# One 512-column matmul for hi and lo of the activation, in the second half of a two-block transformer kernel

## The chip, the core and the metric

The kernel runs on one core of one Trainium2 chip. The metric is the device time of one execution in microseconds. The profile is one further execution, taken by the hardware profiler; its span is from the first to the last instruction. Engines are named as in the profile: PE is TensorE's matmuls, PEld its weight loads, DVE is VectorE, ACT ScalarE, POOL GpSimd, SP SyncE.

## What is computed

Two transformer blocks follow each other on 256 tokens of width 1024, all in float32. The first has two attention layers with cross attention to a memory. The second, which the change touches, is cut to this:

```python
def second_block(x, mem, ...):
    x = x + hybrid_mixer(rms_norm(x, g_mix), w_in, conv_w, g_attn_out, g_conv_out, w_out)
    x = x + memory_cross_attention(rms_norm(x, g_xattn), rms_norm(mem, g_mem),
                                   w_q_mem, w_kv_mem, w_o_mem)
    x = x + squared_relu_mlp(rms_norm(x, g_mlp), w_up, w_down)
    return rms_norm(x, g_final)

def hybrid_mixer(h, w_in, conv_w, g_attn_out, g_conv_out, w_out):
    q, k, v, bg, cg, xc = jnp.split(h @ w_in, 6, axis=-1)
    ...
    conv = short_gated_conv(bg, cg, xc, conv_w)
    merged = jnp.concatenate([rms_norm(attn, g_attn_out), rms_norm(conv, g_conv_out)], axis=-1)
    return merged @ w_out

def squared_relu_mlp(h, w_up, w_down):
    a = jax.nn.relu(h @ w_up)
    return (a * a) @ w_down
```

The mixer's attention has 8 heads of 64 and three dilated windows; cross attention has 4 heads of 256 over 256 memory rows; the MLP is 4096 wide.

## The kernel before

**Numbers in two parts.** Every matmul operand is split into hi (the value rounded to the format fp32r) and lo (what is left). A product takes three matmuls, in `mm3` (L421): hi x hi, hi x lo, lo x hi, all added up in one PSUM bank. Weights are loaded in raw pieces (`load`, L408), and `split` (L413) makes hi with a copy on ACT (tile `wh`) and lo with a subtraction on DVE (tile `wl`), four buffers of each.

**Two forms of projection.** `proj_t` (L427) gives the result transposed, features on the partitions and the 256 tokens on the free axis. It covers 256 features as two halves f of 128. For each half and each of the 8 k tiles of 128 input features it does one `mm3` whose stationary operand is a 128x128 tile of weights and whose moving operand is the activation's hi or lo of 256 columns. Both halves lie in one PSUM bank of 128 x 2 x 256, and the consumers read that bank. `proj_n` (L439) takes the activation as stationary operand and weights of up to 512 columns as moving operand; it gives values and outputs with the tokens on the partitions.

**The activation's tiles.** `turns` (L614), `gain_t` (L478) and `layer_even` (L956) make the normed activation, transposed, as hi and lo. Each returns a function of (l, k) that gives hi (l = 0) or lo (l = 1) of k tile k as 128 x 256. The tiles are slots of 4 KB a partition from a common pool of 25 (`SLOTS`), each with four k tiles of one part: tiles `mT`, `gh` and `hT` in the profile.

**The second block.** `mixer` (L1154) first lets `heads8` (L1063) project k and q (4 calls of `proj_t`) and v; then come the three gates of the convolution, 2 x 3 calls, whose results are multiplied, filtered with three taps, squared and normed; the output projection of the convolution's half and that of the attention's half close it. The sum of squares over tokens (`token_rms`, a reduction on DVE and two small matmuls with a vector of ones) stands between the convolution and its residual add. `filling` (L817) holds the keys and values of the second memory, eight steps that are put where TensorE would wait; two key steps run before the mixer, two at its start. `cross` (L1204) calls `proj_t` for four heads. `mlp` (L1252) runs its first block of 512 features with its own loop (`up_first`), the other seven with two calls of `proj_t` each into PSUM banks of the tag "at" (`up`), while `down` adds into four banks of the tag "mm" that stay open to the end.

**What sets the order.** The program is not issued as it is written. `Plan.record` (L83) notes each operation with its dependences and a cost, and `Plan.order` (L162) simulates the engines: at each step the engine that can start first takes the ready operation with the least priority number (its place in the program, with shifts from `SHIFT`). Buffers are handed out in the order of first use. The result is a fixed order for each engine, so all instructions are issued from one helper and carry its line, L284. In PSUM a dependence is on the whole bank; in SBUF on the part that is read. Work that is put off with `later` is stepped by `pace`, which `proj_t` calls after every fourth k tile.

Of the kernel before, what the change touches and what calls it, by code (L numbers as in the profile page):

```python
# [13 lines left out]
ALU = mybir.AluOpType  # L14
AX = mybir.AxisListType

P = 128
S = 256
D = 1024
KT = D // P  # L20
# [9 lines left out]
class Plan:  # L30
# [5 lines left out]
    class Engine:  # L36

        def __init__(self, plan, name):
            self.plan, self.engine = plan, name
# [244 lines left out]
            f(*[self.real(v) for v in args], **{k: self.real(v) for k, v in kwargs.items()})  # L284


class Kernel:

    def __init__(self, ctx, tc, a, out):
        self.tc, self.nc, self.a, self.out = tc, Plan(tc.nc), a, out  # L290

        class Pool:

            def __init__(pool, name, bufs, space=None):
                pool.space = space
                pool.real = ctx.enter_context(tc.tile_pool(name=name, bufs=bufs, **({"space": space} if space else {})))

            def tile(pool, shape, dtype, tag=None, name=None, bufs=1):
                return self.nc.tile(pool, shape, dtype, tag, name, bufs)

        pool = Pool
        self.base = pool("base", 1)
        self.wp = pool("wp", 4)
        self.wk = pool("wk", 2)
        self.bp = pool("bp", SLOTS)
        self.ps = pool("ps", 2, space=bass.MemoryType.PSUM)
        self.dr = pool("dr", 1, space=bass.MemoryType.DRAM)
        self.n = 0
        self.bg = deque()
        self.credit = 0.0  # L310
        self.rate = 0.0

    def name(self, s):
        self.n += 1
        return f"{s}_{self.n}"
# [4 lines left out]
    def slot(self, shape, name, dtype=F32R):  # L320
        return self.bp.tile(shape, dtype, tag="b4", name=self.name(name), bufs=SLOTS)

# [104 lines left out]
    def proj_t(self, w, c0, hT, n=256, tag="mm"):  # L427

        raw = self.load(w, 0, KT, c0, n)
        po = self.psum(tag)  # L430
        for f in range(n // P):
            wh, wl = self.split(raw[:, :, f * P:(f + 1) * P])
            for k in range(KT):
                self.mm3(po[:, f, :], wh[:, k, :], wl[:, k, :], hT(0, k), hT(1, k), k == 0, k == KT - 1)
                if k % 4 == 3:
                    self.pace()
        return po[:, :n // P, :]

    def proj_n(self, pieces, nk, n, hT, banks=None, start=True, stop=True):  # L439

        nc = self.nc
        po = banks or [self.psum("mm", [P, 512]) for _ in range(2)]
        for k0, view in pieces:
            wh, wl = self.split(view)
            for t in range(2):
                ts = slice(t * P, (t + 1) * P)
                for j in range(view.shape[1]):
                    k = k0 + j
                    o = po[t][:, :n]
                    xh, xl = hT(0, k)[:, ts], hT(1, k)[:, ts]  # L450
                    nc.tensor.matmul(o, xh, wh[:, j, :], start=start and k == 0, stop=False)
                    nc.tensor.matmul(o, xh, wl[:, j, :], start=False, stop=False)
                    nc.tensor.matmul(o, xl, wh[:, j, :], start=False, stop=stop and k == nk - 1)
                self.pace()
        return po
# [22 lines left out]
    def gain_t(self, src, key):  # L478

        nc = self.nc  # L480
        tiles = [[self.slot([P, 4, S], "gh") for _ in range(2)] for _ in range(2)]

        def turn(k):
            v, g, h, l = src[k // 4][:, k % 4, :], self.gcol(key, k), f(0, k), f(1, k)
            nc.scalar.activation(h, v, AF.Copy, scale=g)
            nc.vector.scalar_tensor_tensor(l, v, g, h.bitcast(F32), ALU.mult, ALU.subtract)

        f = lambda l, k: tiles[l][k // 4][:, k % 4, :]
        return f, turn

    def spread(self, r, b):

        nc = self.nc
        diag = self.work("p", [P, 2, P], PB)
        pb = self.psum("at")
# [83 lines left out]
    def mem_key(self, h, l, po, m):  # L579

        t = self.work("p", [P, 2, S], PB)
        self.nc.vector.tensor_tensor(t, po, m[2].unsqueeze(1).to_broadcast([P, 2, S]), ALU.mult)
# [23 lines left out]
    def square_sum(self, v, ms):  # L606

        junk = self.work("p", [P, 512], PB)
        self.nc.either(("scalar", "activation", (junk, v, AF.Square), {"scale": 1.0 / 32.0, "accum_out": ms}),
# [4 lines left out]
    def turns(self, tag, halves, key):  # L614

        nc = self.nc
        tiles = [[None, None], [None, None]]

        def turn(c, k2):
            if k2 == 0:  # L620
                for l in range(2):
                    tiles[l][c] = self.slot([P, 4, S], "mT")
            pt = self.psum("at")
            for j in range(2):
                k = 2 * k2 + j
                for t in range(2):
                    nc.tensor.transpose(pt[:, j, t * P:(t + 1) * P], halves[c][:, t, k * P:(k + 1) * P], self.ident)
            for j in range(2):
                k = 2 * k2 + j
                g = self.gcol(key, 4 * c + k)  # L630
                h, l = tiles[0][c][:, k, :], tiles[1][c][:, k, :]
                nc.scalar.activation(h, pt[:, j, :], AF.Copy, scale=g)
                nc.vector.scalar_tensor_tensor(l, pt[:, j, :], g, h.bitcast(F32), ALU.mult, ALU.subtract)

        for c in range(2):
            for k2 in range(2):
                self.later(tag, lambda c=c, k2=k2: turn(c, k2))
        return lambda l, k: tiles[l][k // 4][:, k % 4, :]


    def hilo(self, h, l, po, scale=1.0):
# [63 lines left out]
    def softmax(self, sc, bias=None, sink=None, causal=False):  # L705
# [3 lines left out]
        n = [P, S] if causal else [S, S]  # L709
        p = self.work("p", [P, 2, S], PB)  # L710
        st = self.work("st", [P, 8], 8)
# [39 lines left out]
    def pv_pair(self, ws, vs, causal=False):  # L751
# [4 lines left out]
        for e, ((ph, pl), v) in enumerate(zip(ws, vs)):  # L756
            for k in range(2):
                q = slice(P, S) if causal and k else slice(0, S)
                nc.tensor.matmul(po[:, e, q], v(k), ph[:, k, q], start=k == 0, stop=False)
                nc.tensor.matmul(po[:, e, q], v(k), pl[:, k, q], start=False, stop=k == 1)  # L760
        u = self.work("y", [P, S], YB)
        o = self.work("y", [P, S], YB)
        for e in range(2):
# [16 lines left out]
    def gated(self, y, f, o, g):  # L780
        nc = self.nc
        t = self.work("y", [P, S], YB)
        nc.vector.scalar_tensor_tensor(t, o, 0.5, g[:, f, :], ALU.mult, ALU.mult)
# [124 lines left out]
    def rope(self, tag, po, n, i, rx):  # L908
# [15 lines left out]
        def turn(t):  # L924
            src, r = po[t][:, :n * 64], rs[t]
            z = self.work("p", [P, 8, 64], PB)
            nc.vector.scalar_tensor_tensor(z[:, :n, :], src.rearrange("p (h c) -> p h c", c=64), rx[:, t:t + 1],
# [28 lines left out]
    def layer_even(self):  # L956
        nc, a = self.nc, self.a
# [20 lines left out]
        po = self.proj_n(pieces(), KT, 384, xg)  # L978
# [3 lines left out]
        nc.vector.tensor_tensor(sq[0], sq[0], sq[1], ALU.add)  # L982
        r = self.token_rms(sq[0])
        rb = self.spread(r, self.work("y", [P, S], YB))
        tiles = [[self.slot([P, 4, S], "hT") for _ in range(2)] for _ in range(2)]
        for c in range(2):
            t = self.slot([P, 4, S], "xs", F32)
            for k in range(4):
                nc.vector.scalar_tensor_tensor(t[:, k, :], self.xT[c][:, k, :], self.gcol("norm0", 4 * c + k), rb,
                                               ALU.mult, ALU.mult)  # L990
            for k in (0, 2):
                self.hilo(tiles[0][c][:, k:k + 2], tiles[1][c][:, k:k + 2], t[:, k:k + 2])
        hT = lambda l, k: tiles[l][k // 4][:, k % 4, :]
        self.window_bias()
        vs = []
        for c0 in (128, 256):
# [144 lines left out]
    def token_rms(self, sq):  # L1141

        nc = self.nc
        s = self.work("y", [P, S], YB)
        nc.vector.tensor_reduce(s, sq.rearrange("p r s -> p s r"), AX.X, ALU.add)
# [8 lines left out]
    def mixer(self, hT):  # L1154
# [22 lines left out]
        for i in range(2):  # L1177
# [8 lines left out]
            for f in range(2):  # L1186
                ff = 2 * i + f
                acc = self.work("y", [P, S], YB)
                tap = lambda j: self.gcol("convw", 4 * j + ff)
# [62 lines left out]
    def mlp(self, ms):  # L1252
# [11 lines left out]
        def square(t, f, n, po):  # L1264
            r = self.work("tanh", [P, 2, S], 2)[:, :n]
            nc.scalar.activation(r, po, AF.Relu)
            q = self.work("p", [P, 2, S], PB)[:, :n]
            nc.scalar.activation(q, r, AF.Square)
# [64 lines left out]
    def run(self, upto=99):  # L1333
        a = self.a
        self.consts()
        ms = self.layer_even()
        if upto > 1:
            ms = self.layer_odd(ms)
        if upto > 2:
            ms = self.mixer(ms)  # L1340
        if upto > 3:
            ms = self.cross(ms)

        def store(c):
            cs = slice(512 * c, 512 * c + 512)
            self.nc.sync.dma_start(self.out[0, :, cs].rearrange("(t p) d -> p t d", p=P), self.x[:, :, cs])

        if upto > 4:
            self.mlp(ms)
        else:  # L1350
            for c in range(2):
                store(c)
        seq = self.nc.solve()
        with self.tc.manual_schedule():
            self.nc.issue(seq)
# [6 lines left out]
BIAS = [40, 80, 110, 0, 0]  # L1362
VERBOSE = False
LAG = (3, 1)
SLOTS = 25
YB = 5
PB = 4
PH = 4
IDLE = [1, 2, 1]
# [79 lines left out]
```

## Time and profile before

| | us |
|---|---|
| median of 3 runs (lowest to highest) | 787.56 (786.85 to 789.11) |
| the profiled execution | 786.07 |
| its span | 784.3 |
| mixer's main stretch, in the span | 390 to 490 |
| cross attention | 510 to 572 |
| MLP from the second block of features on | 600 to 784 |
| mean granted TensorE clock | 0.997 of full speed |

How to read it: a busy time is the time in which at least one instruction of a group was under way. Matmuls overlap each other, so the "mean ns" of a matmul is its latency from issue to last result; the price of one more in a stream is the distance from one start to the next, seen in the timeline or in long runs of the chain of waits. A group's row gives out<-in by tile names, partitions x elements, the count, busy time and mean, and then the idle time before. Idle time of an engine on which nothing waits costs nothing.

### The profile page before, as it was taken

How to read it: one execution, taken by the hardware profiler on the slowest of the kernel's cores; microseconds unless marked ns; L12 is line 12 of the kernel's file. 1: busy time of each engine (PE TensorE's matmuls, PEld its weight loads, DVE VectorE, ACT ScalarE, POOL GpSimd, SP SyncE). 2: the span in 40 equal slices, each digit the busy share in tenths (PEclk: the TensorE clock that was granted, in tenths of full speed). 3: DMA queues.
4: the chain of work that ended last, by engine and by line, in shares of the span. 5: the costliest groups of instructions: out<-in, count | busy, mean ns of one | idle time of the engine just before them, and what ended most of it. 6: DMA issues, size and time to landing. Idle time of an engine off the chain costs nothing.

```text
span 784.3 us, 13568 instructions
## 1 busy us (share of the span) xinstructions
PE 769.9 (98%) x5320; PEld 715.2 (91%) x5320; DVE 578.2 (74%) x995; ACT 506.3 (65%) x928; POOL 74.7 (10%) x105
## 2 busy tenths in 40 slices
PE   7999999999999999999999999999999999999996
PEld 7799899888999999997999899799989999999985
DVE  5999988998769779869987788876567554445454
ACT  6687965975668568648785777465456654455452
POOL 0640010000001521132011000100000000000000
PEclk9999999999999999999999999999999999999999
DMA  7795455444468855773456644357435656565631
GB/s 229 243 333 163 161 166 195 151 159 164 161 198 260 220 175 156 196 233 135 151 172 191 187 159 164 107 162 242 161 108 168 201 170 203 171 208 170 205 116 54
DMA packets 109996, 140.60 MB, mean 179 GB/s; under 512 B 3779, under 2 KB 81539, under 8 KB 109932
## 3 DMA queue, kind: packets, MB, share of 16 engines
q1 hardware_dynamic: 104460, 131.64, 52.0%
q0 software_dynamic: 5472, 8.10, 4.6%
q8 instruction: 42, 0.69, 0.4%
q14 instruction: 22, 0.18, 0.1%
HBM read 134.98 MB, written 1.06 MB: 173 GB/s over the span
## 4 chain that ended last, share of the span: by engine, by line
PE 88%; DVE 4%; issue 3%; POOL 2%; DMA 1%; ACT 1%; SPq 0%; POOLq 0%; DVEq 0%; ACTq 0%
PE t_mm L284 66%; PE t_at L284 22%; DVE t_wl L284 1%; POOL t_rrs L284 1%; DMA t_xT<-in_x_t_dram 1%; DVE t_y L284 1%; DVE t_p L284 1%; POOL t_ks L284 1%; DMA t_tanh<-in_onehot_dram 0%; SPq L284 0%; ACT t_wh L284 0%; POOL t_rstd L284 0%; DVE t_gh L284 0%; DVE t_sq L284 0%; ACT t_tanh L284 0%
## 5 line engine op out<-in xcount | busy, mean ns | idle before, releaser
L284 DVE TENSOR_TENSOR t_wl<-t_raw,t_wh 128x1024 fp32r<-128x1024 f32 (+1 forms) x237 | 290.6, 1230 | 144.8 <-ACT t_wh L284 144.2
L284 ACT ACTIVATE t_wh<-t_raw 128x1024 fp32r<-128x1024 f32 (+1 forms) x237 | 249.0, 1055 | 200.1 <-PE t_mm L284 141.8
L284 PE MATMUL t_mm<-t_mT,t_wh 128*128 128x256 f32 x992 | 192.5, 287 | 0.0
L284 PEld LDWEIGHTS t_mm<-t_mT,t_wh 128*128 128x128 f32 x992 | 159.4, 191 | 0.4
L284 PE MATMUL t_mm<-t_mT,t_wl 128*128 128x256 f32 x496 | 141.1, 285 | 0.0
L284 PE MATMUL t_mm<-t_wh,t_yh 128*128 128x512 f32 x288 | 113.6, 395 | 0.0
L284 PE MATMUL t_mm<-t_wl,t_yh 128*128 128x512 f32 x288 | 113.6, 394 | 0.0
L284 PE MATMUL t_mm<-t_wh,t_yl 128*128 128x512 f32 x288 | 113.1, 394 | 0.0
L284 PE MATMUL t_at<-t_mT,t_wh 128*128 128x256 f32 x480 | 97.0, 282 | 0.0
L284 PEld LDWEIGHTS t_mm<-t_mT,t_wl 128*128 128x128 f32 x496 | 95.0, 191 | 0.0
L284 PEld LDWEIGHTS t_at<-t_mT,t_wh 128*128 128x128 f32 x480 | 78.8, 190 | 1.6
L284 PE MATMUL t_mm<-t_wh,t_gh 128*128 128x256 f32 (+2 forms) x256 | 65.6, 339 | 2.5 <-ACT t_wh L284 2.5
L284 PE MATMUL t_at<-t_mT,t_wl 128*128 128x256 f32 x240 | 67.6, 282 | 0.0
L284 PE MATMUL t_mm<-t_hT,t_wh 128*128 128x256 f32 x336 | 66.4, 287 | 0.0
L284 PEld LDWEIGHTS t_mm<-t_wh,t_yl 128*128 128x128 f32 x288 | 54.1, 188 | 10.6
L284 PEld LDWEIGHTS t_mm<-t_wl,t_yh 128*128 128x128 f32 x288 | 54.2, 188 | 10.0
L284 PEld LDWEIGHTS t_mm<-t_wh,t_yh 128*128 128x128 f32 x288 | 54.2, 188 | 9.7
L284 ACT ACTIVATE t_p<-t_p,t_st 128x256 f32<-128x256 f32 (+1 forms) x118 | 55.9, 490 | 7.4 <-DVE t_st L284 7.1
L284 POOL TENSOR_TENSOR t_rstd<-t_rstd,t_mhalf 128x2 f32<-128x2 f32 (+1 forms) x12 | 12.2, 1015 | 477.4 <-DVE t_rstd L284 477.4
L284 PEld LDWEIGHTS t_mm<-t_hT,t_wh 128*128 128x128 f32 x336 | 54.2, 191 | 0.3
L284 PE MATMUL t_mm<-t_gh,t_wh 128*128 128x256 f32 x256 | 51.1, 287 | 0.0
L284 PEld LDWEIGHTS t_mm<-t_wh,t_gh 128*128 128x128 f32 x256 | 44.6, 193 | 6.9 <-ACT t_wh L284 3.5
(173 smaller groups left out, 1317.6 us busy)
## 6 DMA issues: line engine op xcount, KB each, us to landing
t_raw<-in_w_in_odd_dram SPq DMA_DIRECT2D x20, 1024.0 KB, 5.1
t_raw<-in_w_up_dram SPq DMA_DIRECT2D x16, 1024.0 KB, 5.5
t_raw<-in_w_down_dram SPq DMA_DIRECT2D x16, 1024.0 KB, 5.2
t_raw<-in_w_in_dram SPq DMA_DIRECT2D x12, 1024.0 KB, 5.2
t_raw<-in_w_in_even_dram SPq DMA_DIRECT2D x10, 1024.0 KB, 5.2
t_raw<-in_w_mem_kv_dram SPq DMA_DIRECT2D x8, 1024.0 KB, 5.4
t_raw<-in_w_out_even_dram SPq DMA_DIRECT2D x6, 1024.0 KB, 5.0
t_raw<-in_w_out_odd_dram SPq DMA_DIRECT2D x6, 1024.0 KB, 5.1
```

The costliest lines, as they stand in the source:

```text
L284: f(*[self.real(v) for v in args], **{k: self.real(v) for k, v in kwargs.items()})
```

## The change

In the second block the activation's hi and lo lie side by side, 2 x 256 columns, and go through hi of the weights as one matmul of 512 columns; lo of the weights still takes hi of the activation alone, 256 columns. The flag `merge` is set ahead of the mixer, so the first block keeps `mm3`. A half f now fills a whole bank: the first 256 columns hold hi x hi + lo x hi, the other 256 hold hi x lo. ACT copies the second part to SBUF (tile `sum`, two buffers of 128 x 2 x 256), DVE adds the first part to it, and consumers read the sum from SBUF. A call takes two PSUM banks in turn instead of one. The class `Halves` makes the activation's tiles: two k tiles with both parts each, made when first asked for. The pool has one slot less.

```diff
+class Halves:
+    def __init__(self, make):
+        self.make, self.tiles = make, {}
+    def pair(self, k):
+        if k // 2 not in self.tiles:
+            self.tiles[k // 2] = self.make()
+        t = self.tiles[k // 2]
+        return t[:, :, 0, :], t[:, :, 1, :]
+    def __call__(self, l, k):
+        return self.pair(k - k % 2)[l][:, k % 2, :]
+    def both(self, k):
+        self.pair(k - k % 2)
+        return self.tiles[k // 2][:, k % 2].rearrange("p l s -> p (l s)")
...
     def proj_t(self, w, c0, hT, n=256, tag="mm"):
         raw = self.load(w, 0, KT, c0, n)
+        if self.merge:
+            return self.proj_sum(raw, hT, n, tag)
         po = self.psum(tag)
...
+    def proj_sum(self, raw, hT, n, tag):
+        nc = self.nc
+        s = self.work("sum", [P, 2, S], SB)
+        for f in range(n // P):
+            wh, wl = self.split(raw[:, :, f * P:(f + 1) * P])
+            po = self.psum(tag)
+            pf = po.rearrange("p a b -> p (a b)")
+            for k in range(KT):
+                last = k == KT - 1
+                if last:
+                    nc.tensor.matmul(po[:, 0, :], wl[:, k, :], hT(0, k), start=False, stop=False)
+                nc.tensor.matmul(pf, wh[:, k, :], hT.both(k), start=k == 0, stop=last)
+                if not last:
+                    nc.tensor.matmul(po[:, 0, :], wl[:, k, :], hT(0, k), start=False, stop=False)
+                if k % 4 == 3:
+                    self.pace()
+            nc.scalar.copy(s[:, f, :], po[:, 1, :])
+            nc.vector.tensor_tensor(s[:, f, :], po[:, 0, :], s[:, f, :], ALU.add)
+        return s[:, :n // P, :]
...
-        tiles = [[self.slot([P, 4, S], "gh") for _ in range(2)] for _ in range(2)]
+        f = Halves(lambda: self.slot([P, 2, 2, S], "gh"))
...
             ms = self.layer_odd(ms)
+        self.merge = True
...
-SLOTS = 25
+SLOTS = 24
 YB = 5
+SB = 2
```

`turns` and `layer_even` get `Halves` in the same way, for the tiles `mT` and `hT`.

What the change makes of TensorE's order, in the MLP, within a half of 128 features. A row names the PSUM bank's tile, the activation's tile, the weight tile and the columns. Before, two k steps:

```order
L284 MATMUL t_at_7949<-t_mT_7168,t_wh_7939 128x256
L284 MATMUL t_at_7949<-t_mT_7178,t_wh_7939 128x256
L284 MATMUL t_at_7949<-t_mT_7168,t_wl_7947 128x256
L284 MATMUL t_at_7949<-t_mT_7168,t_wh_7939 128x256
L284 MATMUL t_at_7949<-t_mT_7178,t_wh_7939 128x256
L284 MATMUL t_at_7949<-t_mT_7168,t_wl_7947 128x256
```

Now the last four k steps of a half and the first matmul of the next:

```order
L284 MATMUL t_at_7962<-t_mT_7109,t_wh_7943 128x512
L284 MATMUL t_at_7962<-t_mT_7109,t_wl_7953 128x256
L284 MATMUL t_at_7962<-t_mT_7109,t_wh_7943 128x512
L284 MATMUL t_at_7962<-t_mT_7109,t_wl_7953 128x256
L284 MATMUL t_at_7962<-t_mT_7122,t_wh_7943 128x512
L284 MATMUL t_at_7962<-t_mT_7122,t_wl_7953 128x256 x2
L284 MATMUL t_at_7962<-t_mT_7122,t_wh_7943 128x512
L284 MATMUL t_at_7989<-t_mT_7008,t_wh_7967 128x512
```

The two matmuls of hi of the weights (tiles 7168 and 7178 are hi and lo of the activation) have become one of 512 columns; the steps alternate 512 and 256 columns, in the last step lo of the weights comes first, and the next half begins in a bank of its own.

The second place is VectorE at the end of the mixer's convolution, from the last gate (bg) to the sum of squares. `t_y` are the taps' result and its product with the gate, `t_yl` lo of the normed input of the output projection, `t_wl` its weights. Before:

```order
L284 TENSOR_TENSOR t_wl_6092<-t_raw_5899,t_wh_6058 128x1024
L284 TENSOR_TENSOR t_y_6102<-t_mm_6019,t_y_6056 128x256
L284 TENSOR_TENSOR t_y_6107<-t_mm_6019,t_y_6062 128x256
L284 TENSOR_TENSOR t_wl_6112<-t_raw_5899,t_wh_6096 128x1024
L284 SCALAR_TENSOR_TENSOR t_yl_5835<-t_y_6102,t_gT,t_yh_5824 128x256
L284 SCALAR_TENSOR_TENSOR t_yl_5835<-t_y_6107,t_gT,t_yh_5824 128x256
L284 TENSOR_REDUCE t_y_6132<-t_sq_5831 128x256
```

Now:

```order
L284 TENSOR_TENSOR t_sum_5938<-t_mm_5934,t_sum_5938 128x256
L284 SCALAR_TENSOR_TENSOR t_y_5957<-t_tanh_5677,t_gT,t_y_5957 128x256
L284 TENSOR_TENSOR t_wl_5986<-t_raw_5784,t_wh_5943 128x1024
L284 SCALAR_TENSOR_TENSOR t_yl_5699<-t_y_5968,t_gT,t_yh_5686 128x256
L284 TENSOR_TENSOR t_y_5999<-t_sum_5938,t_y_5957 128x256
L284 TENSOR_TENSOR t_wl_6003<-t_raw_5784,t_wh_5976 128x1024
L284 SCALAR_TENSOR_TENSOR t_yl_5699<-t_y_5999,t_gT,t_yh_5686 128x256
L284 TENSOR_REDUCE t_y_6018<-t_sq_5690 128x256
```

The product reads the sum in SBUF and no longer the bank; the add of the second half and the last taps come first, and the two products stand apart, the first of them ahead of these rows.

More of the change, by code (lines that the diff above doesn't have):

```diff
@@ L311, in __init__ @@
         self.rate = 0.0
+        self.merge = False
     def name(self, s):
@@ L486, in turn @@
             nc.vector.scalar_tensor_tensor(l, v, g, h.bitcast(F32), ALU.mult, ALU.subtract)
-        f = lambda l, k: tiles[l][k // 4][:, k % 4, :]
         return f, turn
@@ L616, in turns @@
         nc = self.nc
-        tiles = [[None, None], [None, None]]
+        f = Halves(lambda: self.slot([P, 2, 2, S], "mT"))
         def turn(c, k2):
-            if k2 == 0:
-                for l in range(2):
-                    tiles[l][c] = self.slot([P, 4, S], "mT")
             pt = self.psum("at")
@@ L630, in turn @@
                 g = self.gcol(key, 4 * c + k)
-                h, l = tiles[0][c][:, k, :], tiles[1][c][:, k, :]
+                h, l = f(0, 4 * c + k), f(1, 4 * c + k)
                 nc.scalar.activation(h, pt[:, j, :], AF.Copy, scale=g)
@@ L637, in turns @@
                 self.later(tag, lambda c=c, k2=k2: turn(c, k2))
-        return lambda l, k: tiles[l][k // 4][:, k % 4, :]
+        return f
     def hilo(self, h, l, po, scale=1.0):
@@ L984, in layer_even @@
         rb = self.spread(r, self.work("y", [P, S], YB))
-        tiles = [[self.slot([P, 4, S], "hT") for _ in range(2)] for _ in range(2)]
+        hT = Halves(lambda: self.slot([P, 2, 2, S], "hT"))
         for c in range(2):
@@ L991, in layer_even @@
             for k in (0, 2):
-                self.hilo(tiles[0][c][:, k:k + 2], tiles[1][c][:, k:k + 2], t[:, k:k + 2])
-        hT = lambda l, k: tiles[l][k // 4][:, k % 4, :]
+                self.hilo(*hT.pair(4 * c + k), t[:, k:k + 2])
         self.window_bias()
```

## Prediction

> **What bounds the kernel now.** I read the head of the page first, then the table of waits for TensorE alone, then the busy time by stretches.
>
> ```profile
> span 784.3 us, 13568 instructions
> PE 769.9 (98%) x5320; PEld 715.2 (91%) x5320; DVE 578.2 (74%) x995; ACT 506.3 (65%) x928; POOL 74.7 (10%) x105
> PE 88%; DVE 4%; issue 3%; POOL 2%; DMA 1%; ACT 1%; SPq 0%; POOLq 0%; DVEq 0%; ACTq 0%
> ```
>
> TensorE is busy 98% of the span and is 88% of the chain that ended last. A page's busy time can hide short gaps, so the waits come next:
>
> ```profile
> PE t_mm L284 <- ACT t_wh L284: 2.5, 1, 2.5
> PE t_at L284 <- DVE t_p L284: 2.0, 4, 1.0
> PE t_at L284 <- POOL t_warm L284: 1.3, 1, 1.3
> PE t_at L284 <- DMA t_tanh<-in_onehot_dram: 0.8, 1, 0.8
> PE t_mm L284 <- DVE t_wl L284: 0.6, 2, 0.4
> ```
>
> That is all: 7.2 us in 784. So what shortens TensorE's own stream shortens the kernel, and what only loads another engine costs nothing until TensorE has to wait for it. The stretches that the change touches (columns: length, PE, PEld, DVE, ACT and POOL busy, clock, DMA share, GB/s):
>
> ```profile
> 390.00:490.00 100.00, 100.00 (x766) 96.44 (x764) 81.43 (x167) 72.47 (x151) 7.55 (x11) 1.00 0.59 179
> 510.00:572.00 62.00, 62.00 (x504) 61.23 (x504) 40.00 (x58) 35.70 (x63) 1.28 (x2) 1.00 0.55 179
> 600.00:784.00 184.00, 177.24 (x1132) 160.80 (x1130) 93.70 (x99) 96.74 (x128) 1.82 (x3) 1.00 0.51 166
> ```
>
> Mixer, cross attention, MLP: TensorE full at a granted clock of 1.00, VectorE at 81%, 65% and 51% (in the last row TensorE's missing 6.8 us lie behind its last matmul, at the program's end).
>
> **The change part by part. 1: fewer matmuls.** Three groups of the second half (from 388 us) hold what is paired, the products of hi of the weights with hi and with lo of the activation:
>
> ```profile
> L284 PE MATMUL t_at<-t_mT,t_wh 128*128 128x256 f32 x480 | 97.0, 282 | 0.0
> L284 PE MATMUL t_mm<-t_mT,t_wh 128*128 128x256 f32 x480 | 92.1, 287 | 0.0
> L284 PE MATMUL t_mm<-t_gh,t_wh 128*128 128x256 f32 x64 | 11.9, 285 | 0.0
> ```
>
> These are 1024; the MLP's first block (up_first, 2 x 32) keeps its own loop, so 960 matmuls of 256 columns become 480 of 512. That is 30 calls: 2 of keys, 10 in the mixer, 4 in cross attention, 14 in the MLP, each with two halves of 8 k steps.
>
> The mean ns in these rows are latencies; the price is the distance from start to start. The chain of waits has unbroken runs (start, length, count):
>
> ```profile
> 651.85 4.44 PE t_at L284 x37
> 755.45 16.36 PE t_mm L284 x72
> ```
>
> 256 columns: 4.44/37 = 120 ns. 512 columns: 16.36/72 = 227 ns. Twice 120 is 240, so a matmul carries 240 - 227 = 13 ns that do not grow with its columns, and a pair made one saves 13. The new stream alternates 512 with 256 columns, and the MLP has such stretches already, where the planner wove two products together:
>
> ```profile
> 637.41 0.40 PE L284 MATMUL t_mm<-t_wh,t_yh 128*128 128x512 f32 x1
> 641.30 0.40 PE L284 MATMUL t_mm<-t_wh,t_yl 128*128 128x512 f32 x1
> ...
> 659.99 0.40 PE L284 MATMUL t_mm<-t_wh,t_yh 128*128 128x512 f32 x1
> 663.81 0.39 PE L284 MATMUL t_mm<-t_wh,t_yl 128*128 128x512 f32 x1
> ```
>
> Each time 11 steps of 512 and 256 lie between the two rows: 3.89/11 = 354 ns and 3.82/11 = 347 ns. A k step costs three times 120 = 360 now, so it saves 6 to 13 ns. I take the middle, 10 ns: 480 x 10 = **4.8 us gained** (2.9 to 6.2). Whether the 13 ns belong to the matmul or to loading its weights makes no difference, for both go.
>
> The Trainium skill has a rule against this ("TensorE: Matmul & The Clock Gate", section "Back-to-back issue gap"): start to start is the columns at the array clock plus about 2.5 ns. By it a pair saves 2.5 ns and 480 pairs 1.2 us. The runs above, with 13 ns, do not agree, and the sum goes by them.
>
> **2: two new steps behind each half.** ScalarE copies the lo bank half to SBUF, VectorE adds the other. Nearest rows of the same shape and memories:
>
> ```profile
> L284 ACT COPY t_rb<-t_at 128x256 f32<-128x256 f32 x2 | 0.7, 374 | 0.6 <-PE t_at L284 0.6
> L284 DVE TENSOR_TENSOR t_y<-t_mm,t_y 128x256 f32<-128x256 f32 x4 | 1.5, 419 | 0.2 <-PE t_mm L284 0.2
> L284 ACT ACTIVATE t_p<-t_tanh 128x512 f32<-128x512 f32 x14 | 8.8, 632 | 0.4
> L284 ACT ACTIVATE t_tanh<-t_at 128x512 f32<-128x512 f32 x14 | 8.1, 581 | 0.0
> ```
>
> 60 copies at 374 ns are 22.4 us of ScalarE, 60 adds at 419 ns are 25.1 us of VectorE; consumers that now read SBUF cost ScalarE 632 - 581 = 51 ns more each, some 30 times, 1.5 us. None of it is on TensorE. By stage: the mixer's stretch (with the key calls 12) gains 12 x 2 x 0.419 = 10.1 us of VectorE, 91.5 in a stretch that shrinks by 192 x 10 ns to 98.1: 93%. Cross attention goes to 40.0 + 3.4 of 62, the MLP to 93.7 + 11.7 of 184; those two I put at nothing, with TensorE's stream as their cover. If that cover failed, each call would show its new latency, 0.374 + 0.419 = 0.8 us. Is 93% too much? Stretches of before that were as full:
>
> ```profile
> 50.00:100.00 50.00, 49.07 (x366) 46.25 (x364) 46.13 (x80) 39.99 (x85) 1.63 (x1) 1.00 0.61 194
> 80.00:90.00 10.00, 10.00 (x55) 8.44 (x54) 9.77 (x18) 9.94 (x26) 0.00 (x0) 1.00 0.47 160
> ```
>
> VectorE at 92% over 50 us went with 0.93 us lost by TensorE (some of it start-up), and 10 us at 98% with ScalarE at 99% lost none. Over 100 us that bounds the loss at 0 to 1.9; I take **0.5 us lost**, near the second row since splits run ahead of TensorE by up to four buffers.
>
> **3: the join at the mixer's end.** The one place where TensorE already waits for a chain out of a projection. There the last conv gate is multiplied, squared, summed (VectorE), and TensorE needs the sum:
>
> ```profile
> 488.88 1.22 DVE L284 TENSOR_TENSOR t_wl<-t_raw,t_wh 128x1024 fp32r<-128x1024 f32 x1
> 490.13 0.76 DVE L284 TENSOR_TENSOR t_y<-t_mm,t_y 128x256 f32<-128x256 f32 x2
> 491.94 0.87 DVE L284 SCALAR_TENSOR_TENSOR t_yl<-t_y,t_gT,t_yh 128x256 fp32r<-128x256 f32 x2
> 492.73 2.01 DVE L284 TENSOR_REDUCE t_y<-t_sq 128x256 f32<-128x1024 f32 x1
> ...
> 488.95 0.28 PE L284 MATMUL t_mm<-t_mT,t_wl 128*128 128x256 f32 x1
> 494.31 0.39 PE L284 MATMUL t_mm<-t_wl,t_yh 128*128 128x512 f32 x1
> 494.80 0.61 PE L284 MATMUL t_at<-t_ones,t_y 128*128 128x1 f32 x4
> ```
>
> From 494.31 the next could start at 494.54; it starts at 494.80: 0.26 lost. In the new order 29 matmuls of 512 stand there instead of 24, 6.6 us of cover after the last projection matmul's 0.23. VectorE's queue in that time, by these rows: the last matmul to its end 0.40, the copy 0.37, add 0.42, a convolution tap 0.48 (like the lo steps, two of which took 0.87 here), wl 1.22, lo 0.48, product 0.42, wl 1.22, lo 0.48, reduction 2.01: 7.5 us. 7.5 - 6.8 = 0.7 against the 0.26 of before, 0.4 more, without the handovers between engines, which no row prices. Below stands 0, since the gate's first half is now out some 2.8 us (8 x 0.35) before its second; above 1.5, if copy and add come on top of all that (0.4 + 0.8) with the handovers. I take **0.7 us lost**, between the row's sum and the upper end. Behind the sum on TensorE wait the conv half's last matmuls, and on VectorE the residual adds.
>
> **4: at nothing.** The hi/lo layout changes addresses, not instructions. One slot fewer: TensorE's order is the same up to the first pair (its row 2704), so nothing ahead of some 395 us moves; behind it, what the slot delays lies under TensorE's stream, and if it does not, it costs one wait of the size above (0.4 to 2.5 us). GpSimd's and SyncE's orders, the transfers among them, are unchanged.
>
> **Sum:** 4.8 - 0.5 - 0.7 = 3.6 us. The profiled execution took 786.07 and should take 782.5. The median of the runs, 787.56, lies 1.5 above that execution; against it I predict **784.0**, the likeliest's own range 781.4 (the 13 ns everywhere, nothing given back) to 786.4 (6 ns, 1.7 given back).
>
> **The rivals.** *No change that can be told.* The pairs save 6 ns as in the 354-ns stretch, 2.9 us, and crowding and join take their upper ends, 3.4: +0.5, 788.1. For it: the two stretches differ though they hold the same instructions. Against: it needs the low end of the first term and the high ends of both losses at once. The skill's 2.5 ns would end here too: 1.2 less 1.2, 787.6.
>
> *Slower: VectorE's queue in the mixer becomes the bound.* VectorE runs in order, and each add sits ahead of the splits (wl) and softmax work that TensorE needs. If at each of the 12 calls there TensorE waits out copy and add, 0.8 us, the mixer loses 9.6 and the time is 787.6 - 4.8 + 9.6 = 792.4. It decides from 0.6 us a call (7.2 us lost: slower by more than 0.3%). For it: the 93%, and the 2.0 us that TensorE already waits for t_p, the softmax weights. Against: the row at 80 us with both engines full and no loss.
>
> *That nothing is merged* has no room: the new order has 480 matmuls fewer on TensorE.
>
> **Chances.** 0.3% of 787.6 is 2.4 us, about what a measurement of this kernel can tell from no change. Forecast, with the better end in it, 0.62; its weak end and the first rival fall within 2.4 us, 0.21; slower 0.17, the second rival. Range 781.2 to 789.6: it takes in the first rival's 788.1 and leaves out most of the second and a sliver below.
>
> **What would show it.** Right: runs of 512 and 256 columns in the MLP at 347 to 354 ns a step; each MLP block 0.3 us shorter; VectorE near 93% between 390 and 490 with TensorE still at 100; the wait before the first sum of squares after the mixer under 1.5 us. Wrong: steps at 360, TensorE below 97% in the mixer, or new waits of TensorE on t_wl, t_p or t_yh of more than 2 us together.

## The result and the profile after

| | before, us | after, us | ratio, 95% interval |
|---|---|---|---|
| first comparison, medians of 6 and 6 runs | 787.20 (785.24 to 789.11) | 782.90 (781.12 to 785.23) | 0.9955 [0.9936, 0.9973] |
| the same kernels on another chip (run e7 below), 9 and 5 runs | 786.82 (785.73 to 787.20) | 781.48 (781.28 to 781.63) | 0.9936 [0.9923, 0.9948] |
| the profiled execution | 786.07 | 782.50 | |
| its span | 784.3 | 780.7 | |

The kernel is 4.3 to 5.3 us faster; 784.0 was predicted. The head of the page after, and the table of TensorE's waits (us in total, times, longest):

```profile
span 780.7 us, 12691 instructions
PE 767.1 (98%) x4840; PEld 691.3 (89%) x4840; DVE 602.0 (77%) x1062; ACT 518.2 (66%) x981; POOL 75.4 (10%) x105
PE 88%; DVE 5%; issue 2%; POOL 2%; DMA 1%; ACT 1%; SPq 0%; POOLq 0%; ACTq 0%; DVEq 0%
```

```profile
PE t_at L284 <- DVE t_p L284: 2.1, 4, 1.0
PE t_mm L284 <- ACT t_wh L284: 1.7, 1, 1.7
PE t_at L284 <- POOL t_warm L284: 1.3, 1, 1.3
PE t_mm L284 <- DVE t_wl L284: 1.2, 3, 0.5
PE t_at L284 <- DVE t_y L284: 0.2, 1, 0.2
```

480 matmuls fewer (5320 - 4840), TensorE still 98% busy, and its waits add up to 6.5 us after 7.2: no wait took the place of the work removed. The groups of the second half with the columns kept apart, and the groups of the tile `sum` (count, durations in ns):

```profile
L284 PE MATMUL t_mm<-t_mT,t_wh 128*128 128x512 f32 x224 | 80.8, 401 | 0.0
L284 PE MATMUL t_at<-t_mT,t_wh 128*128 128x512 f32 x224 | 79.7, 396 | 0.0
L284 PE MATMUL t_mm<-t_gh,t_wh 128*128 128x512 f32 x32 | 11.2, 399 | 0.0
```

```profile
L284 ACT COPY t_sum<-t_mm x32: 344/373/432, 401.0 to 567.5; 128x256 f32<-128x256 f32 x32
L284 DVE TENSOR_TENSOR t_sum<-t_mm,t_sum x32: 410/424/426, 401.5 to 568.4; 128x256 f32<-128x256 f32 x32
L284 ACT COPY t_sum<-t_at x28: 353/373/374, 607.8 to 748.7; 128x256 f32<-128x256 f32 x28
L284 DVE TENSOR_TENSOR t_sum<-t_at,t_sum x28: 418/425/426, 608.2 to 749.1; 128x256 f32<-128x256 f32 x28
```

224 + 224 + 32 = 480 matmuls of 512 columns, 60 copies at 373 ns and 60 adds at 424 ns. The busy time by stretches (columns as before):

```profile
390.00:490.00 100.00, 100.00 (x581) 87.30 (x580) 90.46 (x197) 79.44 (x174) 7.55 (x11) 1.00 0.59 179
505.00:567.00 62.00, 61.95 (x434) 57.71 (x433) 43.98 (x65) 36.71 (x68) 1.29 (x2) 1.00 0.60 193
596.00:780.00 184.00, 177.65 (x922) 151.41 (x920) 107.20 (x129) 104.32 (x159) 1.82 (x3) 1.00 0.51 166
```

VectorE rose from 81% to 90% in the mixer and TensorE is still full there.

**Where the time came from.** TensorE's order of both kernels is the same up to its 2713th matmul, the first pair made one, but the two profiles do not pass there at the same time: the 2691st starts at 392.17 us before, at 392.89 after, and at 391.45 in the second profile of the changed kernel (e7). The difference is there by the 54th matmul (15.22, 16.37, 14.92): scatter of the start-up, 1.4 us between two executions of one kernel. So I measure stages from the 2691st matmul on, between starts of marked matmuls: to the first transpose of cross attention's normed input (`t_xn`), from there to the first transpose of the MLP's (`t_x`), from there to the last matmul, and to the end of the span. Two profiles of one order differ in the last column by 0.1 us (before and e2) and by 0.3 us (the change), so nothing finer is read from it.

| us | start-up scatter: 2691st matmul | mixer and keys | cross attention | MLP | end | from the 2691st on |
|---|---|---|---|---|---|---|
| before | 392.17 | 124.93 | 73.82 | 185.92 | 7.46 | 392.13 |
| after | 392.89 | 123.27 | 73.51 | 183.60 | 7.47 | 387.84 |
| after, second profile (e7) | 391.45 | 123.25 | 73.86 | 183.56 | 7.46 | 388.14 |
| e1, pairs as two matmuls | 392.97 | 124.80 | 74.29 | 186.37 | 7.46 | 392.92 |
| e2, layout alone | 392.03 | 124.78 | 73.82 | 185.94 | 7.51 | 392.05 |
| e3, wide first | 392.45 | 123.01 | 75.38 | 183.40 | 7.40 | 389.18 |
| e4, no add | 392.38 | 123.24 | 73.30 | 183.49 | 7.40 | 387.44 |
| e6, one more VectorE step | 392.00 | 126.29 | 73.60 | 183.74 | 7.46 | 391.08 |
| e9, not in the mixer | 392.77 | 124.79 | 73.27 | 183.56 | 7.46 | 389.08 |

The change gained 4.3 us there in one profile (1.7 in the mixer, 0.3 in cross attention, 2.3 in the MLP) and 4.0 in the other. The 3.6 us between the two spans are 4.3 less 0.7 of start-up.

### The profile page after: what moved, and what is told of

It reads as the page before. It is cut to its first block, busy times and chain, and to the rows that moved or that the text cites. A ratio compares the mean times of both kernels' runs of the same rounds, so it can differ in the third digit from the quotient of the medians.

```text
span 780.7 us, 12691 instructions
## 1 busy us (share of the span) xinstructions
PE 767.1 (98%) x4840; PEld 691.3 (89%) x4840; DVE 602.0 (77%) x1062; ACT 518.2 (66%) x981; POOL 75.4 (10%) x105
## 4 chain that ended last, share of the span: by engine, by line
PE 88%; DVE 5%; issue 2%; POOL 2%; DMA 1%; ACT 1%; SPq 0%; POOLq 0%; ACTq 0%; DVEq 0%
PE t_mm L284 66%; PE t_at L284 22%; DVE t_wl L284 1%; DVE t_y L284 1%; POOL t_rrs L284 1%; DMA t_raw<-in_w_q_mem_dram 1%; DVE t_p L284 1%; DMA t_raw<-in_w_in_even_dram 1%; POOL t_ks L284 1%; ACT t_wh L284 1%; POOL t_rstd L284 0%; DVE t_xs L284 0%; DVE t_hT L284 0%; DVE t_tanh L284 0%; SPq L284 0%
## 5 line engine op out<-in xcount | busy, mean ns | idle before, releaser
L284 PE MATMUL t_mm<-t_mT,t_wh 128*128 128x256 f32 (+1 forms) x768 | 188.3, 320 | 0.0
L284 PE MATMUL t_mm<-t_mT,t_wl 128*128 128x256 f32 x496 | 136.8, 284 | 0.0
L284 PEld LDWEIGHTS t_mm<-t_mT,t_wh 128*128 128x128 f32 x768 | 129.3, 190 | 6.9
L284 PE MATMUL t_at<-t_mT,t_wh 128*128 128x512 f32 (+1 forms) x256 | 85.7, 382 | 0.0
L284 PE MATMUL t_at<-t_mT,t_wl 128*128 128x256 f32 x240 | 63.8, 280 | 0.0
L284 PEld LDWEIGHTS t_mm<-t_wl,t_yh 128*128 128x128 f32 x288 | 54.1, 188 | 10.7
L284 ACT ACTIVATE t_p<-t_p,t_st 128x256 f32<-128x256 f32 (+1 forms) x113 | 53.7, 491 | 5.0 <-DVE t_st L284 4.8
L284 PEld LDWEIGHTS t_at<-t_mT,t_wh 128*128 128x128 f32 x256 | 45.8, 188 | 6.8
L284 PE MATMUL t_mm<-t_gh,t_wh 128*128 128x256 f32 (+1 forms) x224 | 50.4, 304 | 0.0
```

## The experiments

The theory is that of the prediction: a pair made one saves some 10 ns of TensorE's own stream, and the new copies and adds cost only where VectorE has no room or where a chain waits for them. Each ratio is to the kernel before on the same chip; e1, e2, e4 and e6 ran on one chip, e3 and e5 on a second, e7 to e10 on a third.

**e1: the change, with each pair as two matmuls of 256 columns.**

```diff
-                nc.tensor.matmul(pf, wh[:, k, :], hT.both(k), start=k == 0, stop=last)
+                nc.tensor.matmul(po[:, 0, :], wh[:, k, :], hT(0, k), start=k == 0, stop=False)
+                nc.tensor.matmul(po[:, 1, :], wh[:, k, :], hT(1, k), start=False, stop=last)
```

> The change with its banks, copies, adds, tiles and slots, but hi x hi and hi x lo are two matmuls of 256 columns again, 480 more than in the change. Theory (a matmul carries some 10 to 13 ns that do not grow with its columns): TensorE's steps go back to 360 ns, the 4.8 us come back and what the copies and adds cost stays: 787.5 to 788.5 us, ratio to the kernel before 1.000 to 1.002. Rival (the time came from banks freed half by half, from the new tiles or from a luckier order): it stays at 783, ratio 0.9955.

Measured: 788.12 us, ratio 1.0027 [1.0015, 1.0038]. The whole gain is gone and the price of the new steps is left: from the 2691st matmul on 392.92, 5.1 us above the change's 387.84 (4.8 above e7), that is 10.6 (10.0) ns for each of 480 pairs, and 0.8 above before. The MLP shows the same matmul by matmul. In the chain of waits (start, length, count) a half of the new stream and its next period, of the change:

```profile
649.81 5.61 PE t_at L284 x32
671.97 5.61 PE t_at L284 x32
```

and of e1:

```profile
650.34 5.75 PE t_at L284 x48
672.91 5.75 PE t_at L284 x48
```

16 steps of 512 and 256 columns in 5.61 us are 351 ns each; 48 of 256 in 5.75 are 120 ns each, 359 a step. A block's period is 22.16 us against 22.57, 12.8 ns for each of its 32 pairs. So the gain is the merging itself, not the banks, the order or the layout.

**e2: the layout and the smaller pool alone**, the flag `merge` off.

```diff
-        self.merge = True
+        self.merge = False
```

> The kernel before with the new activation tiles and 24 slots; nothing is merged, so no copies, no adds. TensorE's order is that of the kernel before. Theory: the layout is worth nothing, 787.2 us, ratio 0.999 to 1.001. Rival (the layout or the smaller pool has a part in the result): a ratio outside 0.998 to 1.002.

Measured: 787.18 us, ratio 1.001 [1.000, 1.002], and no stage of the table differs from before by more than 0.15 us. Layout and slot cost nothing that the trace shows; the medians leave room for at most 0.2%.

**e4: the copy stays, the add is left out** (so the product of hi of the weights with lo of the activation is not in the result).

```diff
-            nc.scalar.copy(s[:, f, :], po[:, 1, :])
-            nc.vector.tensor_tensor(s[:, f, :], po[:, 0, :], s[:, f, :], ALU.add)
+            nc.scalar.copy(s[:, f, :], po[:, 0, :])
```

> The change without its 60 adds on VectorE; ScalarE copies the first half of the bank alone, so the product of hi of the weights with lo of the activation is left out of the result. It measures what the adds cost. My prediction (0.5 us for a full VectorE in the mixer, 0.7 at the join): 0.5 to 1.2 us faster than the change, 781.7 to 782.4. Rival (the adds lie wholly under TensorE's stream): the change's time, 782.9, within 0.4.

Measured: 781.34 us, ratio 0.9934 [0.9922, 0.9947]; 387.44 from the 2691st on. The time lies below the band that I expected, the stages at its lower end: 22 us less of VectorE (579.6 on its page, 602.0 on the change's) are worth 0.4 us against the change's first profile and 0.7 against its second. In the mixer with its join, where the prediction put the price of the adds, they are worth nothing: 123.24 after 123.27. Of the 0.4 and 0.7, 0.2 and 0.6 lie in cross attention (73.30 after 73.51 and 73.86).

**e6: one more VectorE step behind each half**, a maximum of the sum with itself.

```diff
             nc.vector.tensor_tensor(s[:, f, :], po[:, 0, :], s[:, f, :], ALU.add)
+            nc.vector.tensor_tensor(s[:, f, :], s[:, f, :], s[:, f, :], ALU.max)
```

> The change with one more VectorE operation of 128x256 behind each add (60 in all, some 25 us, results unchanged): VectorE in the mixer's 100 us goes from 90 to 100%. Theory (VectorE costs nothing until it is full): it now is full in the mixer and TensorE waits there, 1 to 6 us slower than the change, all of it between 385 and 500 us; cross attention and MLP, at some 75 and 64%, lose under 0.5. Rival (each step's latency stands in TensorE's path): 30 calls of 0.4 us, 12 us slower, spread over all stages. Third possibility: nothing at all, within 0.5, and VectorE has more room than its busy time says.

Measured: 785.56 us, ratio 0.9987 [0.9979, 0.9996]. The steps took 21 us of VectorE (623.0 on its page, 602.0 on the change's), 0.35 each, and 3.0 us of it show in the mixer, under 0.2 in cross attention and the MLP. Its stretches of mixer and MLP:

```profile
390.00:490.00 100.00, 99.09 (x573) 85.86 (x572) 93.76 (x213) 78.26 (x174) 7.87 (x11) 1.00 0.57 168
596.00:780.00 184.00, 180.01 (x940) 153.63 (x938) 118.15 (x158) 107.09 (x159) 1.81 (x3) 1.00 0.52 168
```

From 81% to 90% VectorE's load cost TensorE nothing that e4 can find; from 90% to 94% a third of what was added (24 steps, 8.4 us) came out on the path. TensorE's new waits between 385 and 500 us are on tiles that VectorE makes, 0.9 us on `t_wl` and 0.4 on `t_mT`, as the slower rival has it. These are two loads in one order: where between them the cost begins was not measured, nor how much of the 3.0 us is the fuller engine and how much the longer chain behind each half.

**e3: in each half the eight matmuls of 512 columns first, then the eight of 256.**

```diff
-                nc.tensor.matmul(pf, wh[:, k, :], hT.both(k), start=k == 0, stop=last)
-                if not last:
-                    nc.tensor.matmul(po[:, 0, :], wl[:, k, :], hT(0, k), start=False, stop=False)
+                nc.tensor.matmul(pf, wh[:, k, :], hT.both(k), start=k == 0, stop=False)
                 if k % 4 == 3:
                     self.pace()
+            for k in range(KT):
+                nc.tensor.matmul(po[:, 0, :], wl[:, k, :], hT(0, k), start=False, stop=k == KT - 1)
```

> The change with each half's eight 512-column matmuls first and its eight 256-column ones behind them. Theory: an alternating step costs 350 ns where 227 + 120 are 347, so 3 ns x 480 = 1.4 us at most are to be had: 781.5 to 782.9. Rival (the price of a step does not depend on the order, and the later need of lo of the weights gives nothing): the change's time within 0.4. If loading other weights at each matmul were the 13 ns, nothing would change either, since each matmul still loads its own.

Measured: 782.23 us, ratio 0.9946 [0.9926, 0.9967]: the change's time. Mixer and MLP are 0.2 to 0.3 us shorter, cross attention 1.9 longer, for one wait that the second profile of the change has too, smaller. ScalarE and TensorE of e3 at the start of cross attention, from the timeline (start, length, what; in brackets the idle time before and what ended it):

```profile
516.48 1.06 ACT L284 ACTIVATE t_wh<-t_raw 128x1024 fp32r<-128x1024 f32 x1 [3.04 <-DMA t_raw<-in_w_q_mem_dram]
517.44 0.70 ACT L284 ACTIVATE t_xn<-t_x,t_rstd 128x512 f32<-128x512 f32 x1
...
518.20 1.64 PE L284 MATMUL t_at<-t_cst,t_xn 128*128 128x128 f32 x13 [2.01 <-ACT t_xn L284]
```

ScalarE of the change, first profile:

```profile
515.21 1.06 ACT L284 ACTIVATE t_wh<-t_raw 128x1024 fp32r<-128x1024 f32 x1 [1.07 <-DMA t_raw<-in_w_q_mem_dram]
516.18 0.71 ACT L284 ACTIVATE t_xn<-t_x,t_rstd 128x512 f32<-128x512 f32 x1
```

and of the kernel before:

```profile
515.67 1.06 ACT L284 ACTIVATE t_wh<-t_raw 128x1024 fp32r<-128x1024 f32 x1 [0.59 <-PE t_mm L284]
516.64 0.71 ACT L284 ACTIVATE t_xn<-t_x,t_rstd 128x512 f32<-128x512 f32 x1
```

In all three the split of the query weights stands ahead of half of the normed input on ScalarE, and the normed input, which needs no transfer, waits with it. The order is not what changed, the transfer is: from its issue on SyncE to its landing it takes 5.4 us before (509.65 to 515.02), and the split then waits for a buffer; it takes 6.4 us in the change's first profile (508.71 to 515.11), 6.7 in the second, 8.4 in e3 (508.01 to 516.38), and the split waits for it. In the change's first profile the wait on ScalarE is 1.07 us and TensorE is covered; in the second it is 1.40 and TensorE loses 0.4; in e3 it is 3.04 and TensorE loses 2.0. The order of SyncE's transfers is the same in all of them. The two ahead of this one are issued 2.71 us apart before, 1.84 in the change and 1.51 in e3; whether that is why it lands later was not tested.

**e5: merged everywhere**, the first block too, 520 pairs more.

```diff
-        self.merge = False
+        self.merge = True
```

> The merged form in the first block too: 520 pairs more, 65 more copies and adds. TensorE's stream loses 520 x 10 ns = 5.2 us; VectorE, at 87 to 92% between 50 and 190 us, gets some 27 us more in the first 390 us. Theory: TensorE gains 5.2, VectorE full in stretches gives back part, 779 to 783 in all. Rival (VectorE becomes the bound where it is over 90% already): 5 to 20 us slower than the change, with TensorE below 97% between 50 and 180 us.

Measured: 780.53 us, ratio 0.9924 [0.9903, 0.9945], in the theory's band; span 777.8, 2.9 below the change's first and 1.8 below its second. At the first transpose of the mixer's input it is 5.2 us ahead of the change's first profile (400.74 against 405.98), which looks like 520 x 10 ns, but 1.4 of that is start-up: it is 3.8 ahead of the second (404.54). Counted from the 54th matmul, e5 is there after 385.8 us and the change after 389.6 in both profiles, 3.9 us ahead; at the first sum of squares after the mixer (477.2 against 478.6) only 1.5 us are left. By the count of lost time that e8 explains, e5 loses 4.0 us more than the change ahead of the mixer's input, 1.6 of them the alternation's own (520 x 3 ns, see there), and 1.2 more from there to the sum of squares. This fits the theory that full engines give part back, and most of it goes in the first block already. Which engine does it there was not tested alone.

**e7: the change once more**, beside the three that follow.

> The changed kernel once more, unaltered, beside the three that follow, so that they are compared with it on one chip. Expected from its first runs: 782.9 us, ratio to before 0.9955, within 0.8 us of the first median. If its first profile's start-up (0.75 us later than before's up to 385 us, in orders that are the same) was scatter, this profile passes 385 us elsewhere, by up to 1 us, and its MLP and mixer have the same lengths to 0.3 us.

Measured: 781.48 us, as in the table at the head; that is 1.4 us below the first median, where I had allowed 0.8, on another chip. The start-up was 1.4 us earlier than in the first profile, MLP and mixer agree to 0.04 us, cross attention took 0.35 more (the wait above).

**e8: merged everywhere but in the mixer and its key calls**, against e5.

```diff
-        self.merge = True
+        self.merge = False
         if upto > 2:
             ms = self.mixer(ms)
+        self.merge = True
```

> Merged everywhere (first block too) except in the mixer with its two key calls. Theory: the merged first block feeds the mixer about 5 us sooner, and what that loses between 402 and 495 us (2.2 us against the change itself) is the copies and adds of the mixer's own calls, on ScalarE and VectorE that have no room there. Without them the loss goes, 2.2 us, and the mixer's price in the change, about 1.0, goes too, against 192 pairs x 10.7 ns = 2.05 us that are not saved: 1 us faster than with all merged (780.5), 779 to 780, TensorE's waits between 400 and 412 us under 0.3 us in all. Rival: the loss there is ScalarE's and VectorE's backlog out of the first block, or the splits, whatever the mixer's calls do: then only the price comes back, and the time is 1 us or more above 780.5, 781.5 to 782.6.

Measured: 781.89 us (779.85 to 782.91), ratio 0.9942 [0.9928, 0.9957]; its span is 777.8, that of e5. The start of the mixer, columns as before, of e5 and then of e8:

```profile
395.00:410.00 15.00, 14.55 (x85) 12.07 (x84) 13.35 (x31) 14.22 (x31) 2.33 (x2) 1.00 0.42 138
```

```profile
395.00:410.00 15.00, 15.00 (x129) 15.00 (x128) 13.31 (x29) 12.97 (x26) 2.33 (x2) 1.00 0.42 138
```

This fits the theory, and of its two engines it points at ScalarE: with the mixer's copies ScalarE is at 95% there and TensorE loses time; without them it is at 86% and TensorE is full, while VectorE stays at 89%. To size it over the stage I took 120, 227 or 109 ns for each matmul by its columns as work and the rest of its distance to the next as lost: from the mixer's first transposes to the sum of squares e5 loses 2.4 us, e8 0.15 (before 0.4, the change 1.2, of which some 170 pairs x 3 ns = 0.5 are the alternation's own, 350 a step where 227 + 120 are 347). But 192 pairs x 13 ns = 2.5 us of work come back, and the two cancel. The 1 us that I expected on top was counted twice: the mixer's price is part of that loss. The time says nothing for the theory either: its median lies in the rival's band.

**e9: the change without the mixer and its key calls.**

```diff
-        self.merge = True
         if upto > 2:
             ms = self.mixer(ms)
+        self.merge = True
```

> The change without the mixer and its two key calls: merged in cross attention, the two other key calls of the second block if they come later, and the MLP alone. The mixer loses 192 pairs x 10.7 ns = 2.05 us of gain and is rid of 24 copies and adds. By the theory that VectorE's crowding and the join cost the mixer 0.8 to 1.2 us in the change: 0.9 to 1.3 us slower than the change, 783.8 to 784.2. By the size that was predicted for crowding and join together (1.2) the lower end, 0.85. Rival, that the whole price of 1.6 us falls in the mixer: 0.4 us slower. Rival, that crowding costs nothing: 2.05 us slower, 785.

Measured: 783.62 us, ratio 0.996 [0.9948, 0.9973]. Against e7 the medians are 2.1 us apart, which alone would speak for crowding that costs nothing; but 1.3 us of the 2.3 between their spans are start-up. From the 2691st matmul on it is 389.08, 1.2 above the change's first profile and 0.9 above e7: the theory's 0.9 to 1.3. Merging in the mixer gains 1.5 us (124.79 - 123.27) of the 2.05 that its pairs save at 10.7 ns each, so 0.5 is given back there; at the prediction's 10 ns it is 0.4.

**e10: merged everywhere, wide first**, the edits of e3 and e5 together.

> Merged everywhere, and in each half first the eight matmuls of 512 columns with hi of the weights, then the eight of 256 with lo. Steps of one kind follow each other at 227 and 120 ns, 347 a pair of them where the alternation took 350: 1000 x 3 ns = 3 us gained at most over 780.5 us; and lo of the weights is wanted 1.8 us later in each half, which gives VectorE room: the 2.2 us that all merged loses between 402 and 495 us shrink below 1. So 776 to 779.5. Rival: ScalarE, not VectorE, is late there (it makes the hi of the weights, which is wanted no later than before, and all eight hi tiles within 1.8 us instead of 2.8): the loss stays or grows, 780 to 782.

Measured: 775.28 us (775.14 to 779.39), ratio 0.9869 [0.985, 0.9888], a little better than the theory's band and the fastest kernel of all: 11.5 us below before, 6.2 below e7 beside it. The first block's stretch and the start of the mixer, of e5:

```profile
50.00:190.00 140.00, 139.37 (x824) 121.06 (x823) 131.61 (x271) 111.65 (x247) 4.57 (x5) 1.00 0.53 171
```

and of e10:

```profile
50.00:190.00 140.00, 139.96 (x832) 122.80 (x831) 129.50 (x264) 116.11 (x259) 4.56 (x5) 1.00 0.53 174
395.00:410.00 15.00, 15.00 (x91) 13.26 (x90) 14.53 (x31) 11.79 (x24) 1.12 (x2) 1.00 0.44 141
```

By the count of lost time above, both kernels have the same work on TensorE (747.6 us); e5 loses 21.5 us over the program, e10 17.2. 2.4 of the 4.3 us lie ahead of the mixer's input, 1.6 from there to the sum of squares. The 3 ns of the alternation are not it: the MLP, with 224 pairs, is only 0.15 us shorter. Two reliefs are left. Lo of the weights, wanted 1.8 us later in each half, would be room for VectorE where it is above 90%. At the mixer's start it was ScalarE that got relief, from 14.22 to 11.79 of 15 us, while VectorE's load rose from 13.35 to 14.53 and TensorE was full all the same. Which of the two does more over the program was not taken apart.

## Why the prediction was right

**The pairs, 4.8 us: right.** e1 against the change gives 5.1 and 4.8 from two profiles, and the step of 351 ns lies between the two stretches of before (354 and 347) from which 10 ns were taken. The rule of the Trainium skill that was weighed there ("TensorE: Matmul & The Clock Gate", section "Back-to-back issue gap"), some 2.5 ns a matmul, which the section gives for a matmul by itself and not for a stream with weight loads, would have made it 1.2 us; the trace, with 13 ns between twice 120 and 227, does not agree.

**The losses, 0.5 + 0.7 = 1.2 us: right in kind, too large, and in part elsewhere.** e1 against before measures all of them at once: 0.8 us from the 2691st matmul on (1.6 between the medians, whose runs hold the start-up's scatter too).

- *Crowding in the mixer, 0.5.* VectorE came to 90%, not 93%, and its adds cost nothing there (e4). What merging gives back in the mixer is 0.2 to 0.5 us all the same (1.9 to 2.05 saved, 1.5 in e9 and 1.7 against before); 0.6 of lost time there is the alternation's own 3 ns (192 pairs), which the 10 ns a pair had already taken in. What the rest is was not shown.
- *The join at the mixer's end, 0.7.* The rows of after that answer to those of before:

```profile
490.60 0.48 DVE L284 SCALAR_TENSOR_TENSOR t_yl<-t_y,t_gT,t_yh 128x256 fp32r<-128x256 f32 x1
491.00 0.42 DVE L284 TENSOR_TENSOR t_y<-t_sum,t_y 128x256 f32<-128x256 f32 x1
491.33 1.22 DVE L284 TENSOR_TENSOR t_wl<-t_raw,t_wh 128x1024 fp32r<-128x1024 f32 x1
...
492.98 1.97 DVE L284 TENSOR_REDUCE t_y<-t_sq 128x256 f32<-128x1024 f32 x1
...
487.86 0.40 PE L284 MATMUL t_mm<-t_mT,t_wh 128*128 128x512 f32 x1
494.46 0.39 PE L284 MATMUL t_mm<-t_wl,t_yh 128*128 128x512 f32 x1
495.00 0.61 PE L284 MATMUL t_at<-t_ones,t_y 128*128 128x1 f32 x4 [0.16 <-DVE t_y L284]
```

From 494.46 the next could start at 494.69; it starts at 495.00: 0.31 lost, 0.26 before. The cover was as forecast (487.86 to 494.69, 6.8 us), the chain was 7.1 us (487.86 to the reduction's end at 494.95) instead of 7.5 plus handovers: on an engine that has work queued, one step starts before the last one's row ends (490.60 + 0.48 is 491.08 and the next starts at 491.00; 491.00 + 0.42 is 491.42 and the next starts at 491.33), so that lengths added up are too much. The join cost 0.05 us more than before.
- *Cross attention and MLP, nothing.* The MLP gained 2.3 us for 224 pairs, 10 ns each: nothing. Cross attention gained 0.3 and then 0.0 of the 0.64 that 64 pairs are worth. In the second profile 0.4 of that is the wait shown at e3, behind a transfer; part 4 rightly had the order of the transfers unchanged and put their landing at nothing. In the first profile TensorE has no such wait, and where the 0.3 went is open.

**By stage** the sum was 0.7 in the mixer (1.9 less 1.2), 0.6 in cross attention and 2.2 in the MLP; measured were 1.7, 0.3 (0.0) and 2.3 (2.4). A loss in the mixer 1 us too large stood against one in cross attention that was not foreseen, and the 0.7 us of a late start-up brought the profiled execution to 782.5, as the sum said. That agreement to a tenth is chance; the agreement of the first term is not.

**The rivals.** No change fell with the 6 ns it needed. The slower one, VectorE bound in the mixer, would have needed 0.6 us a call; the change lost 0.5 us at most over all twelve. e6 shows how near it was: one more step of 0.35 us a half, and 3.0 us are gone.

## What to carry to other kernels

Where TensorE is full and another engine is not, joining two matmuls that share their stationary operand saves the part of a step that does not grow with its columns, here some 10 ns a pair, and the work handed to the others was nearly free here while VectorE stayed at 90% of the stage, and no longer at 94%. That is no fixed limit: in the 15 us around the start of e10's mixer VectorE is at 97% and TensorE is full. Size the gain from start to start in runs of the profile, and look for transfers that land just before they are needed: an earlier TensorE, or a later landing, makes a wait of what queues behind them. Compare stages from a mark behind the start-up, since two executions of one kernel can differ there by a third of what such a change is worth.

## What the runs showed of the hardware

- The start-up scatters by 1.6 us within the first 17 us: over all twelve profiles, whose TensorE order is the same up to the 126th matmul, the 54th starts between 14.92 and 16.49 us; four of them on one chip (e1, e2, e4, e6) between 14.98 and 16.49. From there to the 2691st matmul the nine with the same order take 376.5 to 377.5 us.
- In the alternation a matmul of 256 columns follows one of 512 after 233 ns, and one of 512 follows one of 256 after 117 (medians), where like follows like after 227 and 120. Eight of 512 in a row with a change of weights each time took 227 ns in the banks of tag "at" and 231 in those of tag "mm" (medians, e3 and e10); why was not tried.
- With VectorE at 90% of a 100-us stretch TensorE was busy all 100.00 us, and with it at 94% 99.09 (the change and e6).
